# A transformer layer in split fp32: DMA queue in program order, stores on ScalarE's queue, weights loaded once with two products interleaved, the second norm begun early

## The chip, the cores and the metric

The kernel runs on one core of one Trainium2 chip. The metric is the device time in microseconds of one execution. Engines are named as in the profile: PE (TensorE, with PEld for its weight loads), DVE (VectorE), ACT (ScalarE), POOL (GpSimd), SP (SyncE, which only issues DMAs here).

## The reference

One layer over 512 latent tokens (width 2048) and 256 context tokens. A gated linear attention (4 heads, 128 wide keys, 256 wide values, scans in both directions from the context's final state) and a gated short convolution read the same normed, modulated input. One output projection, a second norm and a SwiGLU FFN with 5632 hidden columns follow, then a final norm. Cut to what matters:

```python
mx = silu(c) @ w_mod + b_mod                  # six rows: sh1, sc1, gt1, sh2, sc2, gt2
hx = rmsnorm(x, norm1_g) * (1 + sc1) + sh1    # the context likewise, from c_ctx
q, k, v, g, lf, lb, cb, cc, cx = split(hx @ w_in)
o = gla_forward(q, k, v, lf) + gla_backward(q, k, v, lb)
mix = concat([rmsnorm_per_head(o) * gla_g * silu(g), cb * conv3(cc * cx)]) @ w_out
x = x + gt1 * mix
h2 = rmsnorm(x, norm2_g) * (1 + sc2) + sh2
x = x + gt2 * ((silu(h2 @ w_ffn_gate) * (h2 @ w_ffn_up)) @ w_ffn_down)
out = rmsnorm(x, final_g)
```

Everything is fp32.

## The kernel before, in words

**Split products.** A product of fp32 matrices is three matmuls of halves (`mm3`, L79 to L84): each operand is split into a rounded half `hi`, made by an ACT copy (L96), and a rest `lo`, made by a DVE subtraction (L97) with both inputs in SBUF. Weights come from HBM as 512 KB tiles `raw` (128 x 1024, four buffers), and are split into `whi` and `wlo` (three buffers each); DVE and ACT do this once for every 12 matmuls of 512 columns.

**Stages**, in the profiled execution. 0 to 150 us: key projection; beside it each chunk of the input is scaled (`scaled_chunk`), whose factors come from small products with the modulation weights (`mod_cols`, tiles `pm`, `tm`, `pc`). 150 to 342: two value passes; the second also makes the shift's share (`shares`). 342 to 425: context states, q, gates. 425 to 875: the four heads, their chunked scan woven with the projections for gate, q and convolution; at each weave step `mod_some(MOD_STEP)` adds rows of the remaining modulation. A row is two 512 KB loads (`raw<-wm`) and two DVE reductions (L363); there are 64 rows. A head ends with a norm whose factors DVE makes in a chain of tiny operations (`rs_m`, `rs_t`, `rs_r`, L136 to L142), then ACT scales (`on`, L623) and PE transposes (`pt`, L629). 875 to 1050: output projection in two blocks of 1024 columns. 1050 to 1150: second norm and the first up block. To 1950: the FFN's 11 gate and up blocks (`wu`). To 2475: the down projection in GROUPS of 6, 6, 6 and 4 pairs of hidden tiles (`wd`), each twice, for the two halves of the columns; the results are added into 16 tiles `y`. Then the final norm and stores.

**Seven products.** From the output projection on, a product of 2 x 2 blocks is made by `seven` (L725 on): seven block products instead of eight, in the order u1 (A11), v (S1), u2 (S2), c12 (S4), u3 (S3), c11 (A12), c21 (A22). `prep_a` makes the left operands: sums and differences of blocks on DVE (tile `s`, L707 to L722) and their splits, named `a0` to `a6`, with `h` and `l`. The right ones are differences made on DVE in the tile `ch` (four buffers, L749 to L762) from weights loaded again for each product: of the eight loads for a unit, block 0 comes once, block 1 twice, block 2 twice, block 3 three times. Between the products, callbacks take the sums from PSUM; in the down stage they are additions `y += acc` on DVE (L974, one input in PSUM), and copies on ACT for the first group (L972). `norm2` runs after the output projection for tokens 0 to 255 and, for the rest, behind the first product of the first up block (`between`).

**Order.** The scheduler that builds the program orders each engine's instructions by their data, their buffers and its own estimates, DMA issues on SP among them; the order in the code is only a starting point. All DMAs, stores too, are issued by SP, which blocks while a target buffer isn't free. SBUF tiles of 2 KB per partition come from `xpool` (72), others from `fpool`; PSUM is three banks for accumulators and five for the rest.

Of the kernel before, what the change touches and what calls it, by code (L numbers as in the profile page):

```python
# [33 lines left out]
GROUPS = (6, 6, 6, 4)  # L34
EPS = 1e-6
# [16 lines left out]
def tile_hybrid_block(  # L52
# [11 lines left out]
    xpool = ctx.enter_context(tc.tile_pool(name="xpool", bufs=72))  # L64
    pspool = ctx.enter_context(tc.tile_pool(name="pspool", bufs=1, space=bass.MemoryType.PSUM))
# [148 lines left out]
    def scaled_chunk(i):  # L214
# [12 lines left out]
        for n, src, acc, dst, q in ((SEQ, xt, saccx, hx, 0), (CTX, ct, saccc, hc, 1)):  # L227
            if q == 0:
                hi, lo = (xpool.tile([P, n], F32R, tag="t", name=name) for name in ("hhi", "hlo"))
# [139 lines left out]
    MOD_STEP = 0.95  # L369
# [49 lines left out]
    for i in range(KD):  # L419
# [256 lines left out]
    fpool = ctx.enter_context(tc.tile_pool(name="fpool", bufs=1, side="right"))  # L676
    A11, S1, S2, S4, S3, A12, A22 = range(7)

    def f2k(name):
        return fpool.tile([P, NB], F32, tag="e", name=name, bufs=8)  # L680
# [4 lines left out]

    def a_unit(A, i, u):
        if A[i][u] is None:
            A[i][u] = tuple(xpool.tile([P, 2, HALF], F32R, tag="t", name=f"a{i}{p}") for p in "hl")
        return A[i][u]

    def prep_a(A, pieces):


        tmp = {}

        def put(n, i, src):
            hi, lo = a_unit(A, i, pieces[n][0])
            split(hi[:, pieces[n][1], :], lo[:, pieces[n][1], :], src)

        tt = nc.vector.tensor_tensor  # L700
        for n, (u, sel, a11, a12, a21, a22) in enumerate(pieces):
            put(n, A11, a11())
        yield
        for n, (u, sel, a11, a12, a21, a22) in enumerate(pieces):
            if u not in tmp:
                tmp[u] = xpool.tile([P, 2, HALF], F32, tag="t", name="s")
            tt(tmp[u][:, sel, :], a21(), a22(), op=ALU.add)  # L707
            put(n, S1, tmp[u][:, sel, :])
        yield
        for n, (u, sel, a11, a12, a21, a22) in enumerate(pieces):  # L710
            t = tmp[u][:, sel, :]
            tt(t, t, a11(), op=ALU.subtract)
            put(n, S2, t)
        yield
        for n, (u, sel, a11, a12, a21, a22) in enumerate(pieces):
            t = tmp[u][:, sel, :]
            tt(t, a12(), t, op=ALU.subtract)  # L717
            put(n, S4, t)
        yield
        for n, (u, sel, a11, a12, a21, a22) in enumerate(pieces):  # L720
            t = xpool.tile([P, 2, HALF], F32, tag="t", name="s3")[:, sel, :]
            tt(t, a11(), a21(), op=ALU.subtract)  # L722
            put(n, S3, t)
        yield
        for n, (u, sel, a11, a12, a21, a22) in enumerate(pieces):  # L725
            put(n, A12, a12())
        yield
        for n, (u, sel, a11, a12, a21, a22) in enumerate(pieces):
            put(n, A22, a22())
        yield  # L730

    def seven(A, wsrc, nk, after, between=lambda n: None):


        nu = nk // 2
        chain = [None] * nu
        tt = nc.vector.tensor_tensor

        def raw(b, u):
            return load_raw(wsrc(b, u))  # L740

        def b11(u):
            r = fpool.tile([P, 2 * NB], F32, tag="ch", name="ch", bufs=4)
            nc.sync.dma_start(r, wsrc(0, u))
            chain[u] = r
            return r

        def t1(u):
            tt(chain[u], raw(1, u), chain[u], op=ALU.subtract)  # L749
            return chain[u]  # L750

        def t2(u):
            tt(chain[u], raw(3, u), chain[u], op=ALU.subtract)  # L753
            return chain[u]

        def t3(u):
            r, r2 = raw(3, u), raw(1, u)
            tt(r, r, r2, op=ALU.subtract)  # L758
            return r

        def t4(u):
            tt(chain[u], raw(2, u), chain[u], op=ALU.subtract)  # L762
            return chain[u]

        X, Y, Z = [], [], []
        plan = (
            ("u1", A11, b11, X, abank, True), ("v", S1, t1, Y, bank, True), ("u2", S2, t2, X, None, False),
            ("c12", S4, lambda u: raw(3, u), Y, None, False), ("u3", S3, t3, X, None, False),
            ("c11", A12, lambda u: raw(2, u), Z, bank, True), ("c21", A22, t4, X, None, False),
        )  # L770
        for n, (name, i, src, acc, alloc, first) in enumerate(plan):
            if first:
                acc += [alloc("acc"), alloc("acc")]
            for u in range(nu):
                r = src(u)
                hi = wpool.tile([P, 1024], F32R, tag="whi", name="whi", bufs=3)
                lo = wpool.tile([P, 1024], F32R, tag="wlo", name="wlo", bufs=3)
                split(hi, lo, r)
                for t in range(2):
                    for k in range(2):  # L780
                        mm3(acc[t], sl(A[i][u], ALL, k, slice(t * P, t * P + P)),
                            (hi[:, k * NB : k * NB + NB], lo[:, k * NB : k * NB + NB]),
                            first and u == 0 and k == 0, u == nu - 1 and k == 1)
            after[name](acc)
            between(n)

    def sums(take):
# [4 lines left out]
        def copied(name):  # L792
            def f(acc):
                s[name] = [f2k(name) for _ in range(2)]
                for t in range(2):
                    nc.scalar.copy(s[name][t], acc[t])
# [16 lines left out]
    def cols_to_row(a, name):  # L813

        pt = bank("ptr")
        nc.tensor.transpose(pt[:KD, :P], modv[:, a : a + KD], ident)
        t = fpool.tile([KD, P], F32, name=name)
        nc.scalar.copy(t, pt[:KD, :P])
        row = tc.dram_tile([1, D], F32, name=name + "d")
        nc.sync.dma_start(row.rearrange("a (k p) -> (a k) p", p=P), t)  # L820
        return row

    def bcast(row, d):
        t = big()
        nc.sync.dma_start(t, row[0, d * NB : d * NB + NB].partition_broadcast(P))
        return t
# [6 lines left out]
    for _ in prep_a(A, [(k // 2, k % 2, mx(8 + k, 0), mx(k, 0), mx(8 + k, 1), mx(k, 1)) for k in range(8)]):  # L833
# [4 lines left out]
    for p in range(NBD // 2):  # L838
        gb = [bcast(gt1d, 2 * p + c) for c in range(2)]
        for tt in range(NX):  # L840
            for c in range(2):
                xn[tt][2 * p + c] = big()
                nc.sync.dma_start(xn[tt][2 * p + c], xr[tt, :, (2 * p + c) * NB : (2 * p + c) * NB + NB])

        def take(tt, c, t, acc):
            d = 2 * p + c
            if t is None:
                t = f2k("g21")
# [272 lines left out]
```

## Time and profile before

| what | value |
|---|---|
| median of the 3 runs shown | 2504.96 us (2496.47 to 2507.55) |
| profiled execution, its own time | 2495.26 us |
| its span | 2492.5 us |
| granted TensorE clock, mean | 0.967 |
| PE busy | 2299.3 us (92%), 10184 matmuls |
| DVE, ACT, POOL busy | 1737.6 (70%), 1029.4 (41%), 72.8 us (3%) |
| moved by DMA | 523.16 MB, 210 GB/s over the span |
| weight loads of 512 KB for output, up and down | 64, 352, 176 |

A row of the timeline gives start, duration, engine, line, operation, out<-in, shape and count; in brackets the idle time just before it and what ended it. A row of the waits gives engine and line, what it waited for, the total, how often, and the longest. A row of a group gives the busy time, the mean in ns, then idle time before. Sums over PE's rows include time at half clock, so a busy PE is not one at full speed; the granted clock tells that apart.

### The profile page before, as it was taken

How to read it: one execution, taken by the hardware profiler on the slowest of the kernel's cores; microseconds unless marked ns; L12 is line 12 of the kernel's file. 1: busy time of each engine (PE TensorE's matmuls, PEld its weight loads, DVE VectorE, ACT ScalarE, POOL GpSimd, SP SyncE). 2: the span in 40 equal slices, each digit the busy share in tenths (PEclk: the TensorE clock that was granted, in tenths of full speed). 3: DMA queues.
4: the chain of work that ended last, by engine and by line, in shares of the span. 5: the costliest groups of instructions: out<-in, count | busy, mean ns of one | idle time of the engine just before them, and what ended most of it. 6: DMA issues, size and time to landing. Idle time of an engine off the chain costs nothing. (4 is left out here: it accounts for less than half of the span.)

```text
span 2492.5 us, 27479 instructions
## 1 busy us (share of the span) xinstructions
PE 2299.3 (92%) x10184; PEld 1806.4 (72%) x10184; DVE 1737.6 (70%) x2140; ACT 1029.4 (41%) x1388; POOL 72.8 (3%) x77
## 2 busy tenths in 40 slices
PE   7899999898989978979999999999999889799996
PEld 4565666777867867767788887887788667687874
DVE  3356255665656488698677876777667677799998
ACT  3333146233222354465444444444444444444443
POOL 2223000000000000000000000000000000000000
PEclk9999999999989999989999999999999989899998
DMA  8655366566756448637666776667666856576684
GB/s 287 220 191 175 110 216 205 195 212 195 234 186 214 132 160 281 217 102 245 215 212 211 253 239 204 215 214 254 225 203 213 262 168 221 186 252 218 223 285 143
DMA packets 183586, 523.16 MB, mean 210 GB/s; under 512 B 18907, under 2 KB 50939, under 8 KB 183324
## 3 DMA queue, kind: packets, MB, share of 16 engines
q1 hardware_dynamic: 183452, 521.42, 64.4%
q8 instruction: 79, 1.29, 0.2%
q14 instruction: 55, 0.45, 0.1%
HBM read 501.40 MB, written 19.94 MB: 209 GB/s over the span
## 5 line engine op out<-in xcount | busy, mean ns | idle before, releaser
L96 ACT CAST whi<-raw 128x1024 fp32r<-128x1024 f32 x318 | 332.2, 1050 | 624.6 <-PE acc L84 327.3
L97 DVE TENSOR_TENSOR wlo<-raw,whi 128x1024 fp32r<-128x1024 f32 x318 | 391.0, 1235 | 255.8 <-ACT whi L96 254.7
L96 ACT CAST whi<-ch 128x1024 fp32r<-128x1024 f32 x296 | 310.5, 1050 | 349.7 <-PE acc L84 251.1
L97 DVE TENSOR_TENSOR wlo<-ch,whi 128x1024 fp32r<-128x1024 f32 x296 | 360.3, 1220 | 90.9 <-ACT whi L96 88.5
L84 PE MATMUL acc<-hhi,wlo 128*128 128x512 f32 x640 | 257.7, 410 | 17.6 <-DVE wlo L97 9.5
L363 DVE CUSTOM_DVE_ANT_0 raw<-raw,cbc 128x1024 f32<-128x1024 f32 x128 | 156.2, 1224 | 166.7 <-DMA raw<-wm 165.1
L84 PE MATMUL acc<-hlo,whi 128*128 128x512 f32 x640 | 256.3, 401 | 0.3 <-DVE hlo L102 0.3
L84 PE MATMUL acc<-hhi,whi 128*128 128x512 f32 x640 | 254.9, 398 | 0.0
L84 PEld LDWEIGHTS acc<-hhi,wlo 128*128 128x128 f32 x640 | 122.3, 192 | 49.9 <-ACT hhi L101 9.0
L84 PEld LDWEIGHTS acc<-hlo,whi 128*128 128x128 f32 x640 | 123.6, 193 | 28.3 <-issue 1.9
L84 PEld LDWEIGHTS acc<-hhi,whi 128*128 128x128 f32 x640 | 123.6, 193 | 27.9 <-issue 1.9
L84 PE MATMUL acc<-whi,a2l 128*128 128x512 f32 x296 | 117.4, 400 | 17.5 <-ACT big L972 10.0
L84 PE MATMUL acc<-whi,a0l 128*128 128x512 f32 x296 | 117.5, 398 | 16.2 <-DVE a0l L97 16.2
L84 PE MATMUL acc<-wlo,a1h 128*128 128x512 f32 x296 | 120.6, 407 | 12.4 <-DVE wlo L97 12.4
L84 PE MATMUL acc<-wlo,a6h 128*128 128x512 f32 x296 | 118.7, 401 | 13.3 <-DVE wlo L97 13.3
L84 PE MATMUL acc<-wlo,a4h 128*128 128x512 f32 x296 | 119.1, 402 | 12.7 <-DVE wlo L97 12.5
L84 PE MATMUL acc<-whi,a4l 128*128 128x512 f32 x296 | 117.0, 399 | 9.5 <-ACT whi L96 6.1
L84 PE MATMUL acc<-wlo,a0h 128*128 128x512 f32 x296 | 118.0, 399 | 8.1 <-DVE wlo L97 8.1
L758 DVE TENSOR_TENSOR raw<-raw 128x1024 f32<-128x1024 f32 x74 | 90.5, 1223 | 47.7 <-DMA raw<-wu 32.3
L84 PE MATMUL acc<-whi,a1l 128*128 128x512 f32 x296 | 118.0, 404 | 5.8 <-DVE a1l L97 3.9
L84 PE MATMUL acc<-wlo,a2h 128*128 128x512 f32 x296 | 117.0, 395 | 2.7 <-DVE wlo L97 2.6
L84 PE MATMUL acc<-whi,a1h 128*128 128x512 f32 x296 | 118.9, 402 | 0.0
(277 smaller groups left out, 4590.7 us busy)
## 6 DMA issues: line engine op xcount, KB each, us to landing
raw<-wu SPq DMA_DIRECT2D x308, 512.0 KB, 4.4
raw<-wd SPq DMA_DIRECT2D x154, 512.0 KB, 4.5
raw<-wm SPq DMA_DIRECT2D x128, 512.0 KB, 4.8
raw<-wo SPq DMA_DIRECT2D x56, 512.0 KB, 4.7
raw<-wc SPq DMA_DIRECT2D x48, 512.0 KB, 4.0
ch<-wu SPq DMA_DIRECT2D x44, 512.0 KB, 5.6
big<-wsc SPq DMA_DIRECT2D x64, 256.0 KB, 6.0
big<-wsh SPq DMA_DIRECT2D x64, 256.0 KB, 5.5
```

Of the source, the lines that this page charges most:

```text
L84: nc.tensor.matmul(o, l, r, start=start, stop=stop, skip_group_check=True)
L96: nc.scalar.copy(hi, src)
L97: (eng or nc.vector).tensor_tensor(lo, src, hi, op=ALU.subtract)
L363: nc.vector.tensor_tensor_reduce(out=w, in0=w, in1=cbc[:, hf * 1024 : hf * 1024 + 1024], scale=1.0, scalar=0.0, op0=ALU.mult, op1=ALU.add, ...
L758: tt(r, r, r2, op=ALU.subtract)
```

## The change

- **Weights once.** `seven` now loads each weight block once per unit, holds the blocks it needs again (`held`, eight buffers), and runs in five steps: "1" is u1, "5" is v, "63" is u2 and c12 interleaved by unit from the same loaded block, "7" is u3, "24" is c11 and c21 interleaved. Loads per unit go from eight to four: 36, 180 and 90 for output, up and down (some blocks run the last step as "2" and "4" apart, which loads block 2 twice). The number of matmuls stays.
- **SP in program order.** The scheduler no longer moves SP's instructions. Stores of the FFN's activations, of the residual (`xnd`) and of two rows go to ACT's queue (62 in all); the output's stay on SP.
- **Modulation rows.** `mod_some(1, 16)` in the second value pass moves 16 of the 64 rows there; `MOD_STEP` goes from 0.95 to 0.7.
- **Output projection.** Its contraction is paired anew (`MIX1`, `MIX2`), so that the first product needs neither the last heads nor the last convolution tiles.
- **Second norm.** Tokens 0 to 255 go through it before step "7" of the second output block, the rest are scaled behind that block and transposed before step "5" of the first up block.
- **Down stage.** The 44 operand sums of its groups are made on POOL, and 82 of the additions into `y` are an ACT copy from PSUM and a POOL addition of two SBUF tiles.
- **Buffers.** PSUM is one pool of eight banks from the output projection on; `xpool` has 56 tiles, `fpool` 17 of its kind; right halves of odd chunks in the first projection use the buffers that later hold `ch`.

```diff
+MIX1, MIX2 = (8, 9, 10, 11, 0, 1, 2, 3), (12, 13, 4, 5, 14, 15, 6, 7)
-    xpool = ctx.enter_context(tc.tile_pool(name="xpool", bufs=72))
+    xpool = ctx.enter_context(tc.tile_pool(name="xpool", bufs=56))
...
-    MOD_STEP = 0.95
+    MOD_STEP = 0.7
...
             for k in ((2 * i - 12, 2 * i - 11) if i < 12 else (i,)):
                 shares(k)
+        mod_some(1, 16)
...
+    ps2 = ctx.enter_context(tc.tile_pool(name="ps2", bufs=8, space=bass.MemoryType.PSUM, reuse_waits="tile"))
...
+        def held(bl, u):
+            r = wpool.tile([P, 2 * NB], F32, tag="ch", name="ch", bufs=8)
+            nc.sync.dma_start(r, wsrc(bl, u))
             return r
...
+        for step in steps:
+            if step in before:
+                before[step]()
             for u in range(nu):
+                end = u == nu - 1
+                if step == "1":
+                    a[u] = held(0, u)
+                    product(A11, u, a[u], X, True)
...
+                elif step == "5":
+                    b[u] = held(1, u)
+                    tt(a[u], b[u], a[u], op=ALU.subtract)
+                    product(S1, u, a[u], Y, True)
...
+                elif step == "63":
+                    d = load_raw(wsrc(3, u))
+                    tt(a[u], d, a[u], op=ALU.subtract)
+                    product(S2, u, a[u], X, False)
...
+                    product(S4, u, d, Y, False)
+                    tt(b[u], d, b[u], op=ALU.subtract)
...
+                elif step == "7":
+                    product(S3, u, b[u], X, False)
...
+                    c = load_raw(wsrc(2, u))
+                    if "2" in step:
+                        product(A12, u, c, Z, True)
...
+                    if "4" in step:
+                        tt(a[u], c, a[u], op=ALU.subtract)
+                        product(A22, u, a[u], X, False)
...
+        before = {"63": load_x}
+        if p:
+            before["7"] = half_a
+        seven(A, lambda b, u: wo[p, b, u], 8, sums(take, True), ("1", "5", "63", "2", "7", "4") if p else ALL_STEPS, before)
...
+        if j == 0:
+            steps, before = ("1", "2", "5", "63", "7", "4"), {"5": half_b}
...
-        nc.sync.dma_start(actd[4 * j + q], t)
+        nc.scalar.dma_start(actd[4 * j + q], t)
...
-        for _ in prep_a(A, pieces):
+        for _ in prep_a(A, pieces, eng=nc.gpsimd):
...
+                        elif fast:
+                            nc.vector.tensor_tensor(o, o, acc[t], op=ALU.add)
                         else:
-                            nc.vector.tensor_tensor(o, o, acc[t], op=ALU.add)
+                            s = big()
+                            nc.scalar.copy(s, acc[t])
+                            nc.gpsimd.tensor_tensor(o, o, s, op=ALU.add)
...
-    with tile.TileContext(nc) as tc:
+    with tile.TileContext(nc) as tc, tc.manual_schedule(engines={mybir.EngineType.SP}):
```

`fast` is the second block of the last group; it keeps its additions on DVE.

**What moves on the engines.** First PE in the key projection, at one of its pairs of chunks: `pm` are the modulation products, `pc` the small one behind the copy `tm`, `acc` with `chl` the context's products, `acc` with `hhi` those of the next scaled chunk. Before:

```order
L84 MATMUL pm<-big,silsh 32x256 x2
L84 MATMUL acc_99<-whi,chl 128x512
L84 MATMUL pm<-big,silsh 32x256 x8
L84 MATMUL pc<-smt,tm 128x2 x2
L84 MATMUL acc_94<-hhi,wlo 128x512
```

and now:

```order
L87 MATMUL pm<-big,silsh 32x256 x2
L87 MATMUL acc_101<-whi,chl 128x512
L87 MATMUL acc_101<-wlo,chl 128x512
L87 MATMUL acc_101<-whi,chl 128x512
L87 MATMUL pc<-smt,tm 128x2 x2
L87 MATMUL acc_100<-whi,chl 128x512
L87 MATMUL acc_101<-whi,chl 128x512
L87 MATMUL acc_96<-hhi,wlo 128x512
```

Three context products have come between the last `pm` and `pc`, and two between `pc` and the next chunk.

Second, DVE at the end of head 0, in the chain that makes the norm's factors; the ISA rows are the reductions of a modulation row. Before:

```order
L136 TENSOR_SCALAR rs_m<-ss 128x4
L138 RECIPROCAL rs_r<-rs_t 128x4
L139 TENSOR_TENSOR rs_t<-rs_r 128x4
L140 TENSOR_TENSOR rs_t<-rs_t,rs_m 128x4
L141 TENSOR_SCALAR rs_t<-rs_t 128x4
L363 ISA raw,modacc<-raw,cbc 128x1024
L363 ISA modacc 128x1
L142 TENSOR_TENSOR rs_r<-rs_r,rs_t 128x4
```

and now:

```order
L139 TENSOR_SCALAR rs_m<-ss 128x4
L141 RECIPROCAL rs_r<-rs_t 128x4
L142 TENSOR_TENSOR rs_t<-rs_r 128x4
L143 TENSOR_TENSOR rs_t<-rs_t,rs_m 128x4
L144 TENSOR_SCALAR rs_t<-rs_t 128x4
L145 TENSOR_TENSOR rs_r<-rs_r,rs_t 128x4
L370 ISA raw,modacc<-raw,cbc 128x1024
L370 ISA modacc 128x1
```

The reduction has gone behind the chain's last step. In head 2 it is the same; in head 1 a reduction stands inside the chain before and now.

Third, ACT at the start of the down stage's third group: `big<-acc` are the copies for the additions into `y`, `a0h` and `a1h` the new group's operands, `whi` its weights:

```order
L1015 COPY big<-acc 128x512 x4
L99 CAST a0h<-ar 128x512 x3
L99 CAST a1h<-s 128x512 x2
L99 CAST whi<-ch 128x1024
L99 CAST a1h<-s 128x512
```

and POOL at the same place:

```order
L1016 TENSOR_TENSOR y<-y,big 128x512 x28
L719 TENSOR_TENSOR s<-ar 128x512 x2
L721 TENSOR_TENSOR s<-s,ar 128x512
L719 TENSOR_TENSOR s<-ar 128x512
```

Before, ACT made no such copies there and POOL had no instruction in this stage: the additions into `y` (L974) and the sums `s` (L707 on) stood on DVE, spread among the weight splits. Now the sums `s` wait on POOL behind all additions of the group before.

More of the change, by code (lines that the diff above doesn't have):

```diff
@@ L790, in sums @@
+    def sums(take, roomy=False):
         s = {}
@@ L793, in f @@
             def f(acc):
-                s[name] = [f2k(name) for _ in range(2)]
+                s[name] = [big() if roomy and name == "v" else row2k(name) for _ in range(2)]
                 for t in range(2):
```

305 lines of the change are left out of this document (150 added, 155 removed).

## The prediction

> **What bounds the kernel now.** I read the page's head first, then the table of stretches that cut the span at the stages' borders, then the list of waits, and last the single rows around the longest waits. The head says that TensorE is the bound, and how nearly:
>
> ```profile
> span 2492.5 us, 27479 instructions
> PE 2299.3 (92%) x10184; PEld 1806.4 (72%) x10184; DVE 1737.6 (70%) x2140; ACT 1029.4 (41%) x1388; POOL 72.8 (3%) x77
> ```
>
> The table of stretches gives, for each, its length, the busy time of PE, PEld, DVE, ACT and POOL with their records, the granted clock, the share of the DMA engines and GB/s:
>
> ```profile
> 16.00:150.00 134.00, 120.05 (x632) 78.17 (x632) 49.58 (x77) 46.49 (x84) 39.16 (x42) 0.95 0.69 223
> 255.00:342.00 87.00, 87.00 (x406) 55.81 (x405) 20.36 (x32) 14.25 (x23) 2.34 (x3) 1.00 0.45 148
> 425.00:875.00 450.00, 408.20 (x1847) 339.31 (x1848) 266.56 (x449) 130.38 (x210) 0.00 (x0) 0.95 0.60 194
> 875.00:975.00 100.00, 79.74 (x322) 62.06 (x321) 83.16 (x133) 49.88 (x92) 0.00 (x0) 0.93 0.65 212
> 1050.00:1150.00 100.00, 80.31 (x359) 64.33 (x358) 92.78 (x136) 59.60 (x93) 0.00 (x0) 0.93 0.50 156
> 1150.00:1950.00 800.00, 790.99 (x3529) 646.73 (x3528) 585.33 (x540) 368.41 (x422) 0.00 (x0) 1.00 0.70 224
> 1950.00:2025.00 75.00, 52.22 (x208) 40.52 (x207) 55.22 (x66) 35.30 (x50) 0.00 (x0) 0.84 0.54 179
> 2025.00:2475.00 450.00, 417.65 (x1743) 334.39 (x1741) 394.14 (x448) 196.70 (x240) 0.00 (x0) 0.96 0.68 222
> ```
>
> Two stages leave nothing to win: the second value pass (255 to 342) and the gate and up blocks (1150 to 1950) have PE busy for 87.0 of 87 and 791.0 of 800 us at full clock. The latter gives the price of a product: 800 us / 3529 records = 0.227 us. What can be won lies where PE idles, and there the clock column falls too: 425 to 875 has 41.8 us of idle and, at 0.95, 450 x 0.05 = 22.5 us more, so an idle microsecond costs 1.54 there. In the down stage (2025 to 2475) it is 32.4 of idle and 18 of clock, 1.56. No stretch fills the DMA engines. So I price the change by idle taken from PE, times some 1.5, and ask of every saved load whether PE or DVE was waiting for it.
>
> **The change part by part.**
>
> *Key projection.* For every pair of chunks PE now waits twice, at the small product behind the modulation and at the next scaled chunk. The list of waits within 16 to 150 sums these:
>
> ```profile
> 94.33 0.61 PE L84 MATMUL pc<-smt,tm 128*128 128x2 f32 x4 [0.55 <-ACT tm L203]
> 96.12 1.36 PE L84 MATMUL acc<-hhi,wlo 128*128 128x512 f32 x4 [1.19 <-ACT hhi L101]
> PE acc L84 <- ACT hhi L101: 8.1, 7, 1.2
> PE pc L84 <- ACT tm L203: 4.3, 8, 0.6
> ```
>
> In the new PE order three context products stand between the last modulation product and the small one (3 x 0.227 = 0.68, more than 0.55), and two behind it (0.45 of 1.19). What remains is 8 x 0.74 = 5.9 of 12.4: 6.5 saved. The clock's loss there is 134 x 0.05 = 6.7; I count 5.5 of it. **+12**, between 6.5 (idle alone) and 19 (both gone).
>
> *Sixteen modulation rows moved into the second value pass.* They are 32 loads of 512 KB in a stretch that moved 148 GB/s x 87 = 12.9 MB, 24 loads. 56 loads are 29.4 MB. The fastest stretch of the trace is
>
> ```profile
> 0.00:50.00 50.00, 35.32 (x214) 20.60 (x215) 16.05 (x23) 17.68 (x32) 10.99 (x21) 0.99 0.94 302
> ```
>
> At 302 GB/s that is 97 us, at the 223 of 16 to 150 it is 132. With only four raw buffers I take 102, i.e. **-15**; -45 at the slow end, 0 if the scheduler's loads spread into the neighbours. DVE's 32 x 1.22 = 39 us of row reductions fit beside its 20.4 busy.
>
> *Attention heads.* All of PE's idle there is in three waits; the first two are
>
> ```profile
> PE pt L629 <- ACT on L623: 20.3, 3, 8.1
> PE psc L84 <- DVE qe L568: 16.4, 6, 4.8
> 513.38 1.22 DVE L363 CUSTOM_DVE_ANT_0 raw<-raw,cbc 128x1024 f32<-128x1024 f32 x1 [2.63 <-DMA raw<-wm]
> 514.53 0.16 DVE L142 TENSOR_TENSOR rs_r<-rs_r,rs_t 128x4 f32<-128x4 f32 x1
> 515.31 0.69 PE L629 MATMUL pt<-cidt,on 128*128 128x128 f32 x2 [5.76 <-ACT on L623]
> 736.30 2.42 PE L629 MATMUL pt<-cidt,on 128*128 128x128 f32 x8 [8.08 <-ACT on L623]
> 847.21 1.03 PE L629 MATMUL pt<-cidt,on 128*128 128x128 f32 x8
> ```
>
> In head 0 a modulation row, itself late by DMA, stands inside the norm's short chain on DVE, just ahead of its last step (L142), and PE waits 5.76 for it. In head 3, where no row is left to load, PE doesn't wait (847.21). The three waits are those of heads 0, 1 and 2. The new DVE order has the chain unbroken in heads 0 and 2 and still broken in head 1, so 5.76 + 8.08 = 13.8 go. Times 1.54 that is 21. DVE loses 39 of its 267 us there, 15%; I let the score waits shrink by as much, 2.4 x 1.54 = 4. **+25**, from 8 (one head, and nothing else) to 50.
>
> *Products of w_out.* Each weight block is loaded once, so the stage needs 36 loads for 64, and the inputs' halves are paired so that the first product needs no late head. But PE's long wait at its start is for DVE, which prepares the operands:
>
> ```profile
> 889.34 0.79 PE L84 MATMUL acc<-wlo,a0h 128*128 128x512 f32 x1 [7.72 <-DVE wlo L97]
> 902.87 0.80 PE L84 MATMUL acc<-wlo,a1h 128*128 128x512 f32 x1 [2.42 <-DVE wlo L97]
> ```
>
> The same operand splits still stand ahead of the third weight split in the new DVE order, so I leave these 10.1 us. The other 10.2 of the 20.3 idle in 875 to 975 I let go, with their share of the clock (7 x 10.2/20.3 = 3.5), less some 2 since all four units' operands of one kind now come in a row: **+12**, 0 to 20.
>
> *Norm begun early.* Its two waits are
>
> ```profile
> 1069.43 5.56 PE L885 MATMUL pt<-cidt,big 128*128 128x128 f32 x32 [5.30 <-ACT big L878]
> 1096.95 0.80 PE L84 MATMUL acc<-whi,a1l 128*128 128x512 f32 x1 [3.94 <-DVE a1l L97]
> ```
>
> Half a's transposes now have 48 products behind them before their result is read, and half b's 96 (A11 and A12). Both waits, 9.2, go; their clock share I set against what moves into the stage ahead: **+9**, -5 to 20.
>
> *Gate and up blocks.* Loads go from 352 to 180, but PE idles 9 of 800 us: **0**, at best +9, at worst -20 if buffers held longer stop something. The 62 stores on ACT's queue I count at nothing, since ACT is busy for 41% of the span; where they stand ahead of a cast that PE waits for, they are part of the -20.
>
> *Down stage.* Here DVE is busy 394 of 450 and PE waits for it. What goes:
>
> ```profile
> 1980.65 0.80 PE L84 MATMUL acc<-whi,a0l 128*128 128x512 f32 x1 [8.39 <-DVE a0l L97]
> 2015.55 0.79 PE L84 MATMUL acc<-whi,a2l 128*128 128x512 f32 x1 [9.97 <-ACT big L972]
> 2122.25 0.80 PE L84 MATMUL acc<-whi,a0l 128*128 128x512 f32 x1 [5.90 <-DVE a0l L97]
> 2140.79 0.47 PE L84 MATMUL acc<-whi,a2l 128*128 128x512 f32 x1 [2.79 <-DVE big L974]
> 2268.65 0.80 PE L84 MATMUL acc<-wlo,a1h 128*128 128x512 f32 x1 [2.25 <-DVE wlo L97]
> 2419.01 0.80 PE L84 MATMUL acc<-wlo,a6h 128*128 128x512 f32 x1 [3.45 <-DVE wlo L97]
> ```
>
> The first group's operands are now split among the last up block's weights; eight shared banks end the waits for a copied bank; the rest belong to group starts, priced anew below. Together 32.7 x 1.56 = 51. DVE is rid of 82 additions into y and 44 operand sums, 126 x 0.68 = 86 us. But POOL takes them, and the two engines block each other:
>
> ```profile
> L974 DVE TENSOR_TENSOR big<-big,acc 128x512 f32<-128x512 f32 x96 | 63.4, 680 | 1.8 <-PE acc L84 1.6
> L97 DVE TENSOR_TENSOR wlo<-ch,whi 128x1024 fp32r<-128x1024 f32 x296 | 360.3, 1220 | 90.9 <-ACT whi L96 88.5
> 199.81 1.29 POOL L294 TENSOR_TENSOR ht<-hhi,hlo 128x512 f32<-128x512 f32 x1 [1.23 <-PE pl L84]
> 199.87 2.32 DVE L97 TENSOR_TENSOR wlo<-raw,whi 128x1024 fp32r<-128x1024 f32 x1
> ```
>
> The split at 199.87, which begins just behind a POOL addition, takes 2.32 instead of its usual 1.22: 1.10 lost. All 126 would cost DVE 139 us. DVE without its additions is busy (394 - 86)/450 = 68%, nearly all of it with two operands in SBUF; I charge 0.68 x 139 = 95, net 9 us more on DVE, x 1.56 = -14. The Trainium skill's page "SBUF — State Buffer", section "Who interferes with whom", states that a VectorE instruction with two SBUF inputs and a GpSimd one that reads SBUF exclude each other for the whole instruction, while one with at most one SBUF input is free. By that rule the additions removed (one input in PSUM) never blocked and those added do; the rows at 199.8 agree.
>
> At the start of groups 2 to 4 the new ACT order has four copies, five operand casts (two of sums that POOL makes behind four y additions) and only then the first weight cast. From the last product: copies 2 x 0.63, one addition and two sums on POOL 3 x 1.29, two casts 1.2, the weight cast 1.05: some 8 us, and 3 x 8 x 1.56 = -37. Stage: 51 - 14 - 37 = **0**. If POOL blocked nothing, the 14 comes back, and with it the 15 us of other waits for weight splits (x 1.56 = 23): +37. If each addition blocks in full, (53 - 9) x 1.56 = -69.
>
> *End.* Row scaling of finished rows stood ahead of the last additions on DVE:
>
> ```profile
> 2474.54 0.39 PE L84 MATMUL acc<-whi,a6h 128*128 128x512 f32 x1
> 2471.81 5.39 DVE L996 SCALAR_TENSOR_TENSOR big<-big,rs_r 128x512 f32<-128x512 f32 x8
> 2477.11 1.28 DVE L974 TENSOR_TENSOR big<-big,acc 128x512 f32<-128x512 f32 x2
> ```
>
> The last product ends at 2474.9, its addition starts at 2477.1; in the new order the finished rows come earlier, and 2.2 us go: **+2**.
>
> Sum: 12 - 15 + 25 + 12 + 9 + 0 + 0 + 2 = 45. The profiled execution took 2495.3 us around its span of 2492.5, 9.7 below the median of the runs shown, 2504.96. So 2450 for it, and **2460** for the median.
>
> **The rivals.**
>
> *POOL's additions block DVE in full.* For it: the pair at 199.8, DVE's 88% in the down stage, and that both engines' operands lie in SBUF. Against: POOL's additions come in groups behind ACT's copies, and some must fall into DVE's waits for casts (88.5 us over all splits of held blocks). The stage loses 69 more: 2529, slower. It decides from 29 us of extra blocking, since 45 / 1.56 = 29, that is when the additions cost 95 + 29 = 124 of 139. The Trainium skill's page "SBUF — State Buffer", in the section named above, has whichever engine starts first hold the other off in full; the trace has four splits beside POOL and no whole stage, so it can't say how often they meet.
>
> *The order of SP takes it back.* Where SP goes in program order and waits for one of four raw buffers, all behind it wait. The second value pass then runs at 223 GB/s (-45 instead of -15), and a head's chain stays as late as its loads (0 instead of 25): 2460 + 30 + 25 = 2515, no change. For it: DVE waits for modulation rows over most of the heads:
>
> ```profile
> DVE raw L363 <- DMA raw<-wm: 165.1, 85, 4.9
> ```
>
> Against: the order on DVE in two heads has no row inside the chain.
>
> *POOL runs beside DVE for nothing.* Then DVE falls to two thirds of the down stage: 2460 - 37 = 2423.
>
> **How the numbers follow.** A measurement of this kernel tells about 0.5%, 12.5 us, from no change. Forecast 0.48 (its own range 2440 to 2488, all faster), full blocking 0.17, SP's order 0.15, free additions 0.20. So faster 0.68, same 0.15, slower 0.17. The range reaches into both sides' cases: 2412 to 2522.
>
> **What would show it.** Right: no wait of several us at the transposes of heads 0 and 2; the second value pass near 100 us with over 280 GB/s; the waits at 1069, 1980, 2015 and 2122 gone; weight splits in the down stage with a mean between 1.4 and 1.8 us instead of 1.22, and some 8 us of idle at the starts of groups 2 to 4. Wrong: a mean above 2 us there (full blocking), a value pass above 120 us, or idle in the blocks of 1150 to 1950, where I expect none.

## The result and the profile after

The changed kernel takes 2571.6 us (2568.3 to 2574.5), the kernel before 2500.7 in the same rounds: a ratio of 1.028, 95% interval 1.025 to 1.031. It is slower; the forecast was 2460, the range 2412 to 2522.

The table of stretches of the changed kernel shows where. Its borders are put where PE has done as much work (each matmul counted with its duration at full clock) as at the borders used before. The columns are those of the prediction's table.

```profile
0.00:191.00 191.00, 152.51 (x671) 90.61 (x672) 57.98 (x84) 49.01 (x93) 42.27 (x47) 0.84 0.55 176
191.00:314.00 123.00, 109.15 (x486) 66.72 (x485) 68.85 (x112) 32.20 (x53) 35.23 (x28) 0.93 0.52 181
314.00:421.00 107.00, 91.66 (x398) 58.45 (x397) 50.42 (x82) 15.28 (x25) 1.05 (x2) 0.89 0.73 247
506.00:920.00 414.00, 398.96 (x1852) 331.91 (x1852) 235.87 (x398) 131.38 (x212) 0.00 (x0) 0.99 0.54 174
2026.00:2573.00 547.00, 428.11 (x1744) 341.01 (x1742) 415.08 (x355) 242.54 (x328) 213.61 (x114) 0.89 0.32 110
```

(Some of these borders lie 1 us beside those of the next table, and the last row leaves out the down stage's first 54 us.)

The lengths of all stages of the two kernels, in us, each from its own profiled execution with borders set in that way, and each rounded by itself:

| stage | before | changed | forecast's gain | measured gain |
|---|---|---|---|---|
| key projection | 150 | 191 | +12 | -41 |
| first value pass | 105 | 122 | none named | -17 |
| second value pass | 87 | 108 | -15 | -21 |
| heads | 450 | 413 | +25 | +37 |
| output projection | 175 | 176 | +12 | -1 |
| second norm, first up block | 100 | 88 | +9 | +12 |
| gate and up blocks | 800 | 789 | 0 | +11 |
| down stage and end | 543 | 600 | +2 | -58 |

The remaining stretch (context states, 83) became 85. Two stretches carry the loss: everything up to the end of the second value pass, 79 us, and the down stage with its end, 58. The gains in between are 59. The two profiled executions lie 79 us apart, the medians 71, so some us of the table are differences between executions of one kernel.

In the heads the three waits at the transposes, 20.3 us in the kernel before, are nearly gone:

```profile
PE pt L637 <- ACT on L631: 3.4, 3, 1.5
```

**The key projection.** PE's timeline of the changed kernel has the same wait once in each pair of chunks, of which three are shown, with the stretches just behind the middle one:

```profile
53.64 1.19 PE L87 MATMUL acc<-whi,chl 128*128 128x512 f32 x2 [2.96 <-DVE chl L105]
74.15 1.19 PE L87 MATMUL acc<-whi,chl 128*128 128x512 f32 x2 [2.88 <-DVE chl L105]
94.06 1.19 PE L87 MATMUL acc<-whi,chl 128*128 128x512 f32 x2 [2.96 <-DVE chl L105]
76.00:78.00 2.00, 2.00 (x6) 1.55 (x5) 1.32 (x1) 0.00 (x0) 1.91 (x2) 0.50 0.53 174
80.00:82.00 2.00, 2.00 (x15) 1.10 (x14) 0.00 (x0) 0.00 (x0) 0.00 (x0) 1.00 0.00 0
```

The period is 19.9 to 20.5 us; before it was about 16.4 (79.68 to 96.12). The wait is 2.9 us where the two waits before made 1.7, and five microseconds at half clock follow it. What PE waits for is `chl`, the scaled context chunk of the *next* pair.

From the first of these waits to the last it is 121.5 us for six periods, where the kernel before took 96.5: 25 of the 41 us. Most of the rest, 14, is lost behind the last wait (35.3 us to the stage's border, 20.9 before). There PE waits for the norm's factors and for the first weights of the next stage:

```profile
171.16 0.71 PE L87 MATMUL pr<-rb_d,cidt 128*128 128x128 f32 x4 [2.32 <-DVE rb_d L152]
175.91 1.22 PE L87 MATMUL acc<-whi,hlo 128*128 128x512 f32 x2 [1.41 <-ACT whi L99]
179.97 0.79 PE L87 MATMUL acc<-wlo,hhi 128*128 128x512 f32 x1 [2.85 <-DVE wlo L100]
```

The loads of these weights were issued at 138 us; their cast stands on ACT behind the copies of the factors (L288), at 174.8. Before, products of the value pass stood between these factors' products, and PE didn't wait.

**The down stage.** PE's waits from the second group on:

```profile
2121.39 1.22 PE L87 MATMUL acc<-whi,a0l 128*128 128x512 f32 x2 [4.21 <-ACT whi L99]
2140.57 0.80 PE L87 MATMUL acc<-wlo,a1h 128*128 128x512 f32 x1 [5.04 <-DVE wlo L100]
2158.85 0.79 PE L87 MATMUL acc<-whi,a2l 128*128 128x512 f32 x1 [6.55 <-ACT big L1015]
2271.82 1.22 PE L87 MATMUL acc<-whi,a0l 128*128 128x512 f32 x2 [7.01 <-ACT whi L99]
2434.57 1.22 PE L87 MATMUL acc<-whi,a0l 128*128 128x512 f32 x2 [19.98 <-ACT whi L99]
2476.03 1.22 PE L87 MATMUL acc<-whi,a5l 128*128 128x512 f32 x2 [7.63 <-ACT whi L99]
2497.11 1.22 PE L87 MATMUL acc<-whi,a0l 128*128 128x512 f32 x2 [8.30 <-ACT whi L99]
2551.06 1.22 PE L87 MATMUL acc<-whi,a6l 128*128 128x512 f32 x2 [17.48 <-ACT whi L99]
```

The first four belong to the starts of groups 2 and 3, which the forecast had priced at 8 us each; they have three waits each (15.8 us in the second group, 18.6 in the third, of which one is shown). The last four, 53 us, are in the last group: its start, priced at 8 as well, and three waits that the forecast had not named. Three lists tell what stands behind the first and the last of them. First ACT at 2414, the start of the last group:

```profile
2414.68 0.58 ACT L1015 COPY big<-acc 128x512 f32<-128x512 f32 x1 [0.77 <-PE acc L87]
2415.16 1.14 ACT L99 CAST a0h<-ar 128x512 fp32r<-128x512 f32 x2
2418.31 0.62 ACT L99 CAST a1h<-s 128x512 fp32r<-128x512 f32 x1 [2.00 <-POOL s L719]
...
2432.43 1.13 ACT L99 CAST a6h<-ar 128x512 fp32r<-128x512 f32 x2
2433.47 1.99 ACT L99 CAST whi<-ch 128x1024 fp32r<-128x1024 f32 x2
```

All 14 operand casts stand ahead of the group's first weight cast, with a wait for a POOL sum before most of them. The waits at 2476 and 2497 end in the same manner: ACT's weight cast stands behind Squares of finished blocks (L1029), which wait for DVE and, through it, for POOL's additions:

```profile
2473.71 0.63 ACT L1029 ACTIVATE big<-y 128x512 f32<-128x512 f32 x1 [3.86 <-DVE y L1028]
2474.95 1.03 ACT L99 CAST whi<-raw 128x1024 fp32r<-128x1024 f32 x1
```

Second SP at the end, and third the groups of POOL's additions and of DVE's weight splits:

```profile
2481.11 0.85 SPq L1026 DMA_DIRECT2D big<-xnd  x2
2536.77 4.97 SPq L1037 DMA_DIRECT2D out<-y  x8
2542.83 0.88 SPq L115 DMA_DIRECT2D raw<-wd  x2
```

```profile
L1016 POOL TENSOR_TENSOR y<-y,big 128x512 f32<-128x512 f32 x82 | 157.2, 1936 | 277.0 <-ACT big L1015 276.5
L100 DVE TENSOR_TENSOR wlo<-ch,whi 128x1024 fp32r<-128x1024 f32 x370 | 478.2, 1300 | 148.5 <-ACT whi L99 147.0
L100 DVE TENSOR_TENSOR wlo<-raw,whi 128x1024 fp32r<-128x1024 f32 x244 | 312.9, 1283 | 108.9 <-ACT whi L99 108.6
```

SP issues nothing between 2482 and 2536.8: it stands at the stores of the first finished rows, whose values are not there yet, and the last two weight loads come behind them. POOL's addition takes 1.94 us in the mean, where the kernel before had 1.29; the splits are 0.06 to 0.08 longer, which is (1.300 - 1.222) x 370 + (1.283 - 1.227) x 244 = 43 us against the kernel with the additions on DVE (below). In the window from 2026 us on alone, the splits take 1.48 us in the mean, within the 1.4 to 1.8 that the prediction had named:

```profile
L100 DVE TENSOR_TENSOR wlo<-ch,whi 128x1024 fp32r<-128x1024 f32 x102 | 151.1, 1486 | 40.5 <-ACT whi L99 40.2
L100 DVE TENSOR_TENSOR wlo<-raw,whi 128x1024 fp32r<-128x1024 f32 x42 | 61.9, 1475 | 25.6 <-ACT whi L99 25.6
```

### The profile page after: what moved, and what is told of

Its sections match the earlier page's. It is cut to its first block, busy times and chain, and to the rows that moved or that the text cites. A ratio compares the mean times of both kernels' runs of the same rounds, so it can differ in the third digit from the quotient of the medians.

```text
span 2572.6 us, 27050 instructions
## 1 busy us (share of the span) xinstructions
PE 2328.3 (91%) x10184; PEld 1820.3 (71%) x10184; DVE 1743.1 (68%) x2014; ACT 1070.9 (42%) x1471; POOL 313.9 (12%) x203
## 5 line engine op out<-in xcount | busy, mean ns | idle before, releaser
L100 DVE TENSOR_TENSOR wlo<-ch,whi 128x1024 fp32r<-128x1024 f32 x370 | 478.2, 1300 | 148.5 <-ACT whi L99 147.0
L719 POOL TENSOR_TENSOR s<-ar 128x512 f32<-128x512 f32 x11 | 18.8, 1715 | 1618.7 <-DMA ar<-actd 1618.7
L87 PE MATMUL acc<-hhl,whi 128*128 128x512 f32 x640 | 201.6, 395 | 0.0
L1016 POOL TENSOR_TENSOR y<-y,big 128x512 f32<-128x512 f32 x82 | 157.2, 1936 | 277.0 <-ACT big L1015 276.5
L87 PE MATMUL acc<-hhi,wlo 128*128 128x512 f32 x320 | 140.1, 438 | 5.5 <-DVE wlo L100 5.5
L87 PEld LDWEIGHTS acc<-hhl,whi 128*128 128x128 f32 x640 | 119.7, 189 | 33.5 <-issue 9.5
L87 PE MATMUL acc<-wlo,a0h 128*128 128x512 f32 x296 | 121.9, 412 | 20.0 <-DVE wlo L100 19.9
L87 PE MATMUL acc<-whi,a6l 128*128 128x512 f32 x296 | 117.1, 397 | 19.3 <-ACT whi L99 17.5
L87 PE MATMUL acc<-hlo,whi 128*128 128x512 f32 x320 | 132.2, 413 | 0.0
L87 PE MATMUL acc<-hhi,whi 128*128 128x512 f32 x320 | 131.2, 410 | 0.0
L87 PE MATMUL acc<-hhl,wlo 128*128 128x512 f32 x320 | 126.6, 395 | 0.0
L87 PE MATMUL acc<-whi,a5l 128*128 128x512 f32 x296 | 117.0, 396 | 7.6 <-ACT whi L99 7.6
```

What stands on the lines that cost most here:

```text
L87: nc.tensor.matmul(o, l, r, start=start, stop=stop, skip_group_check=True)
L100: (eng or nc.vector).tensor_tensor(lo, src, hi, op=ALU.subtract)
L1016: nc.gpsimd.tensor_tensor(o, o, s, op=ALU.add)
```

## The experiments

All edits are to the changed kernel, and all times are medians beside the kernel before (2497 to 2500 in these rounds).

**SP's issues placed by the scheduler.**

```diff
-    with tile.TileContext(nc) as tc, tc.manual_schedule(engines={mybir.EngineType.SP}):
+    with tile.TileContext(nc) as tc:
```

> The changed kernel with one part undone: the scheduler again places SP's DMA issues (no program order on SP). Theory: program order on SP makes the scheduler see the modulation weights of the key projection late, so that PE waits 2.9 us for the context's scaled chunk in every pair (19.9 us a pair) and runs at half clock behind it; and it puts the stores of the first finished rows ahead of the last weight loads, for which PE waits 17.5 us at 2551. Then the part up to the end of the second value pass (421 us in the changed kernel, 342 before) falls by 50 to 80 us, the 17.5 us wait goes, and the time is 2480 to 2510. Rival: the smaller tile pool and the odd chunks' halves in other buffers slow that part; then it stays at 400 us or more, and the time is 2545 to 2575.

Measured 2486.2, ratio 0.996 (0.994 to 0.997): 85 us less. The key projection is at 150 us again, the first value pass at 110; the second stays at 107. The end's wait of 17.5 us is down to 6.2. Its first 150 us read like those of the kernel before (228 GB/s there too, 672 products):

```profile
0.00:150.00 150.00, 127.14 (x672) 82.99 (x672) 55.35 (x85) 53.26 (x95) 39.48 (x47) 0.94 0.70 228
```

So the program order of one DMA queue, and not the tile pools, cost the projections 54 us (41 and 13). The down stage with its end takes 567 us instead of 600; PE's waits above 1.5 us in the last group fall from 56 us to 25, while those at the starts of groups 2 and 3 get no shorter.

**Additions and sums back on DVE.**

```diff
-        for _ in prep_a(A, pieces, eng=nc.gpsimd):
+        for _ in prep_a(A, pieces):
...
-                            s = big()
-                            nc.scalar.copy(s, acc[t])
-                            nc.gpsimd.tensor_tensor(o, o, s, op=ALU.add)
+                            nc.vector.tensor_tensor(o, o, acc[t], op=ALU.add)
```

> The changed kernel with one part undone: the additions into y and the operand sums of the down stage back on DVE, the additions reading PSUM, without ACT copies. Up to the down stage nothing changes. Theory A: what costs there is the serial chain at the starts of groups (copies on ACT, additions on POOL, sums on POOL, then the casts and only then the weight cast), with ACT in order behind it; then the waits at 2121, 2271, 2434, 2476 and 2497 (4.2, 7.0, 20.0, 7.6, 8.3 us) shrink and the time is 2500 to 2530. The 17.5 us wait for the last weights stays. Theory B: the lock between POOL and DVE costs more than the chain; then weight splits fall from 1.30 to 1.22 us, and the time falls by 60 us or more with PE's waits for DVE gone. Rival: the waits at group starts come from SP's program order (late loads); then they stay at 15 us or more in the last group and the time is 2555 to 2575.

Measured 2478.1, ratio 0.992 (0.990 to 0.994): 93 us less, more than theory A gave and within theory B's 60 or more. Down stage and end take 509 us instead of 600. No wait at a group start is above 2.2 us (the one at the start of the last group's second block is 4.3), and the splits are at 1.22. Both theories' signs came, so this run doesn't tell chain and lock apart; the experiments on the additions below do. The last group's wait for its last weights, SP's doing, stayed:

```profile
2116.16 0.50 PE L87 MATMUL acc<-wlo,a1h 128*128 128x512 f32 x1 [2.10 <-DVE wlo L100]
2230.58 0.79 PE L87 MATMUL acc<-wlo,a0h 128*128 128x512 f32 x1 [2.06 <-DVE wlo L100]
2355.09 0.50 PE L87 MATMUL acc<-wlo,a0h 128*128 128x512 f32 x1 [2.20 <-DVE wlo L100]
2453.94 1.22 PE L87 MATMUL acc<-whi,a6l 128*128 128x512 f32 x2 [18.49 <-ACT whi L99]
```

**The first stores behind the last product.** The eight stores of `out[0]` and `out[1]` are moved from `finish_rows` to behind the loop over the groups.

> The changed kernel with the eight stores of the first two finished token tiles issued behind the last product instead of ahead of it. Theory: SP, in program order, waits for these rows (54.7 us) and issues the last two weight loads and residual loads only then; with the stores behind, PE's 17.5 us wait at the end falls below 5 and the time is 2550 to 2560. Rival: the last product waits for DVE's final work anyway, time unchanged within 5 us of 2571.

Measured 2565.7, ratio 1.027 (1.025 to 1.029). The 17.5 us wait fell to 2.6 and a new one of 5.1 for the last split came behind it: ten microseconds off PE, but only 6 off the median, outside the expected 2550 to 2560, and the intervals of the two kernels overlap (1.025 to 1.031 for the changed one). Part of what the stores had held up was late for DVE's sake anyway. So the stores explain at most a part of the 33 us that SP's order costs in the down stage; its effect on the other waits of the last group was not taken apart.

**The modulation rows as before.** `MOD_STEP = 0.95`, and no `mod_some(1, 16)`.

> The changed kernel with the modulation rows as before (none in the second value pass, step 0.95 in the heads). Forecast's step: the moved rows cost the second value pass 15 us and win 25 in the heads. If so the time rises by 5 to 15, to 2580. Theory after the result: the second value pass lost 20.6 us and the heads won 37; undoing gives back 15 to 20 in the pass and takes 20 to 37 in the heads: 2570 to 2590. Rival: the heads won by other parts (SP's order, buffers) and the pass lost by the loads: the time falls by 10 to 20, to 2555.

Measured 2580.3, ratio 1.032 (1.030 to 1.034). The second value pass is back at 86 us, 22 less, and the heads at 447, 34 more. PE's waits at the transposes are back at 17.7 us. The moved rows thus win about 9 us, though the intervals of the two kernels still touch; and nearly all of the 37 us in the heads is theirs.

**Both parts undone.** The first two edits together.

> The changed kernel with both parts undone: SP's issues placed by the scheduler, and the down stage's additions and sums on DVE. Theory: the two costs lie in different stages (SP's order in the projections and at the end, POOL's chain in the down stage), so the gains add: 2571 - 85 - 93 = 2393, within 12. Rival: they share a cost (the last group, where both held weights back), then 2405 to 2440.

Measured 2400.7, ratio 0.961 (0.957 to 0.964): 171 us less where the two gave 85 and 93. The costs are nearly independent.

**The modulation weights one chunk earlier, SP still in program order.** `mod_cols` is cut in two, and its loads for the next pair are issued in the odd chunk ahead:

```diff
+        if i + 1 in sc_at and i > 1:
+            fetch_cols(wsc, i + 1, sc_at[i + 1])
         xt = big()
         nc.sync.dma_start(xt, xT[:, i, :])
```

In the order of PE the small product then has all of the odd chunk's products behind it:

```
MATMUL pm<-big,silsh 32x256 x14
MATMUL pc<-smt,tm 128x2 x2
MATMUL acc_96<-hhl,wlo 128x512
```

> The changed kernel, SP still in program order, but in the program each pair's modulation weights of the key projection are loaded one chunk earlier. Theory: not program order itself but the late place of these loads in it makes the scheduler spread the modulation products and put the small product just before its result is needed. In the order of this kernel the modulation products stand together and a whole odd chunk's products stand behind the small one, so PE's 2.9 us waits in each pair go, the key projection ends at 150 to 160 us instead of 191, and the time is 2530 to 2542. Rival: the 56 tiles limit how far loads run ahead; then the loads wait for tiles, and the key projection stays at 180 us or more.

Measured 2528.4, ratio 1.012 (1.010 to 1.015): 43 us less, and the key projection ends at 151. The waits for `chl` are 6.6 us in all, where the seven of the changed kernel (2.9 each) make 20.4:

```profile
PE acc L87 <- DVE chl L105: 6.6, 7, 2.9
PE pc L87 <- ACT tm L219: 4.2, 8, 0.6
```

So the waits in the pairs came not from program order itself but from the place that these loads had in it. A pair now takes 13.8 us from the second on, less than the 16.1 of the kernel before. Behind the last pair nothing changed: the waits of 2.3, 1.4 and 2.9 us are still there, and this part takes 32 us. With SP's issues scheduled they are absent (22 us for this part), so some 10 us remain a price of program order, by way of the order on ACT.

**The additions alone, the sums alone.** First only the additions into `y` back on DVE, then only the operand sums.

> The changed kernel with the additions into y back on DVE; the operand sums stay on POOL. Theory of the chain: without additions ahead of them, POOL's sums are ready early, ACT has no copies ahead of the casts, and the waits at group starts (15 to 20 us each) go: 2475 to 2500, nearly as with both undone (2478). Rival, lock by count of POOL instructions (82 of 126): two thirds of the 93 us, about 2510.

> The changed kernel with the operand sums back on DVE; the additions into y stay on POOL behind ACT copies. Theory of the chain: the sums no longer queue behind the additions, so the 20 us wait of the last group falls below 8, but copies still stand ahead of the casts and the Square of the last group still waits for POOL: 2520 to 2545. Rival, lock by count (44 of 126): a third of the 93 us, about 2540, with the waits for casts unchanged. If the chain through the sums were all of it, the time would be that with both undone, 2478.

Measured 2489.0 (0.996, 0.994 to 0.998) and 2545.5 (1.019, 1.017 to 1.021). Undone alone, the additions are worth 83 of the 93 us, the sums 26; 44 sums left on POOL cost 11 us (the two kernels' intervals just touch), 82 additions 67. The expectation that the 20 us wait would fall below 8 with the sums on DVE was wrong: it stayed at 18.8. The queue of sums behind additions on POOL was not what held the weight cast.

**POOL's traffic without its place.** Additions and sums on DVE, and behind each addition but the fast block's one on POOL that nobody reads: `nc.gpsimd.tensor_tensor(scratch, o, o, op=ALU.add)`.

> The kernel with both additions and sums on DVE (2478), and behind each of the 82 additions into y one more addition on POOL, of two SBUF operands, whose result nobody reads: POOL's traffic without its place in the chain. If what y's additions on POOL cost (2546 against 2478, 67 us) is the lock between the engines, the time is 2525 to 2550 with weight splits at 1.27 us. If it is the chain of copy, addition and what waits for them, the lock shows in the splits (1.25 to 1.27) and costs at most 20 us: 2478 to 2498.

Measured 2506.2, ratio 1.003 (1.002 to 1.005): 28 us more than without, between the two expectations. The lock in its groups:

```profile
L100 DVE TENSOR_TENSOR wlo<-ch,whi 128x1024 fp32r<-128x1024 f32 x370 | 460.1, 1250 | 121.4 <-ACT whi L99 119.6
L1015 POOL TENSOR_TENSOR scratch<-y 128x512 f32<-128x512 f32 x82 | 127.8, 1559 | 1952.6 <-DVE y L1013 1948.8
```

28 / 82 = 0.34 us of time for each addition, where the prediction's row at 199.87 has a split lose 1.10 beside one.

**The path by copies without POOL.** Sums on DVE, and `nc.vector` in place of `nc.gpsimd` in the addition; the ACT copy stays.

> The changed kernel with sums on DVE and the additions into y on DVE too, but still by way of an ACT copy, from two SBUF operands: the chain's copies without POOL. If the copies ahead of the casts on ACT are what the starts of groups wait for, some 5 us remain at each and the time is 2495 to 2515. If it is POOL's slow additions (1.9 us each) that hold back copies' tiles and the last group's Square, the time is 2470 to 2490.

Measured 2526.2, ratio 1.010 (1.008 to 1.013): 48 us more than with additions straight from PSUM, beyond both expectations. POOL is not needed for the long wait; ACT's order at the last group is the same as in the changed kernel:

```profile
2376.79 0.58 ACT L1015 COPY big<-acc 128x512 f32<-128x512 f32 x1 [0.77 <-PE acc L87]
2377.28 1.14 ACT L99 CAST a0h<-ar 128x512 fp32r<-128x512 f32 x2
2379.94 0.62 ACT L99 CAST a1h<-s 128x512 fp32r<-128x512 f32 x1 [1.53 <-DVE s L719]
...
2392.60 1.13 ACT L99 CAST a6h<-ar 128x512 fp32r<-128x512 f32 x2
2393.64 1.99 ACT L99 CAST whi<-ch 128x1024 fp32r<-128x1024 f32 x2
2394.73 1.22 PE L87 MATMUL acc<-whi,a0l 128*128 128x512 f32 x2 [17.97 <-ACT whi L99]
```

In the kernel whose additions read PSUM, ACT's casts are spread among the weight casts of the group before:

```profile
2326.22 0.61 ACT L99 CAST a0h<-ar 128x512 fp32r<-128x512 f32 x1
2327.98 1.06 ACT L99 CAST whi<-ch 128x1024 fp32r<-128x1024 f32 x1 [1.15 <-PE acc L87]
...
2331.66 0.61 ACT L99 CAST a1h<-s 128x512 fp32r<-128x512 f32 x1
```

With copies, the scheduler puts the next group's operands behind the last copies. Why it does was not tried; its view of ACT's load or of the copies' tiles may decide it.

The kernels so far make a chain in which each differs from the one before by one edit: additions by way of copies, on DVE (2478.1 to 2526.2, 48 us), the same additions on POOL (to 2545.5, 19 us), the sums on POOL as well (to 2571.6, 26 us). Together these are the 93. The parts are sure to some 3 us, since they come from different rounds.

**Program order kept, its costs out.** The edits on the loads, the stores, the additions and the sums together.

> SP still in program order, with the modulation weights of the key projection loaded one chunk earlier, the first finished rows stored behind the last product, and additions and sums on DVE. Gains measured one by one: 43, 6 to 14 and 93 us. If they add: 2571 - 142 to 150 = 2421 to 2429. What then stays above the kernel with SP's issues scheduled (2401) is the first value pass, 12 to 17 us.

Measured 2425.9, ratio 0.971 (0.968 to 0.974), as the single gains add. (Of its parts, the stores' 6 is not clear of noise.) The first value pass is at 121 us against 114 with SP's issues scheduled, and the down stage with its end takes 501 against 485.

**Scheduled, and the loads ahead.** Both parts undone, and the modulation weights one chunk earlier.

> SP's issues placed by the scheduler, additions and sums on DVE (2401), and the key projection's modulation weights one chunk earlier in the program. If their place in the program still decides, the 1.1 us waits of each pair and the half clock behind them go, and the time is 2375 to 2392; if the scheduler places them by itself, 2401 within 8.

Measured 2389.1, ratio 0.956 (0.954 to 0.958), the best version of the study. The key projection takes 137 us; of the 1.1 us waits per pair that were left only the first two remain (1.1 and 1.8). The 14 us to the kernel with these loads ahead and SP in program order (151) are mostly the part behind the last pair, where PE doesn't wait now. The place in the program decides even where the scheduler may move the loads.

## Why the prediction was wrong, by its own steps

**Key projection, +12: the sign was wrong.** The step read the two context products behind `pc` as work of the old chunk that would cover 0.45 us of the next chunk's wait. They belong to the next pair and need its `chl`, which is made behind `gx`, `hhi` and `hlo`; PE meets the chain earlier, not later. A wait of 2.9 us per pair instead of 1.7, followed by half clock, gave 25 of the 41: over the six periods PE idles 17.5 us instead of 11.3, and the granted clock is 0.84 instead of 0.93, some 13 us; what makes the remaining 6 was not measured. The other 14, behind the last pair, were no term of the sum. The names in the order alone did not tell to which pair of chunks a product belongs. Undoing the queue's order brings the stage back to 150 us, moving its loads by one chunk to 151.

**SP in program order.** It was priced only in a rival, and there for the second value pass and the heads. That rival's place was wrong and its mechanism half right: the second pass takes 107 us with and without program order, and the heads won all the same. Undoing it won 41 and 13 us in the projections and 33 in the down stage. For the pairs of the key projection the runs show why: the loads' place. In the last group SP stood for 54.7 us at stores of unfinished rows, but moving these won 6 us, not clear of noise; why the first value pass paid 13 was not tried. What is queued behind each waiting issue on SP should have been read; the forecast did that for ACT and POOL only.

**Second value pass, -15, and heads, +25: right in kind.** -21 and +37. The pass moved 247 GB/s, less than the 280 assumed. The heads' waits at the transposes fell by 16.9 us and not by 13.8: head 1's, which the forecast had left, went as well. The granted clock is 0.99 instead of 0.95. The rows taken out give 34 of the 37, as the run with them put back shows.

**Output projection, +12: -1.** The loads saved were not what PE waited for: its wait for the operands' splits at the start, which the forecast left at 7.7, grew to 12.2 (at 940 us), and its waits in the stage are 24 us in all, as before.

**Norm, +9: +12; gate and up, 0: +11.** The first number is near by luck: of the two waits that were to go, the one for the transposes (5.30) went, but the one for `a1l` (3.94) is still there, 4.39 at 1145.6; shorter waits for splits, which the forecast had not counted, made up for it. In gate and up PE's idle time fell from 9.0 to 3.6 us, and its busy time, which the forecast took as fixed, from 791.0 to 785.4, so the gain is above the 9 that it called the best. No run has the weights loaded again or the norm late with all else kept, so these gains are read off the profiles.

**Down stage, 0: about -58 with the end.** The gains at the first group came (21 us). The step that failed is the group starts at 37 us: it took one order (four copies, five casts, the weight cast) for three groups, 8 us each. For the second and third the first wait was below that price (4.2 and 7.0), but two more of 5 and 6.5 us followed in each; for the fourth the order has 14 casts ahead of the weight cast, which the forecast did not look at, and the wait was 20. The end's +2 was wrong in the same manner: in the last group Squares on ACT and stores on SP stand ahead of weights, 33 us in three waits.

**The lock, -14: right in kind, too small.** The splits' mean in the stage, 1.48 us, is as forecast, and below the 2 us that would have been the sign of full blocking. In time the lock cost more than 14: 28 us for 82 additions (the unread ones), 11 for the 44 sums alone on POOL, 39 together, though the second figure has the sums' own lateness in it. The charge on DVE, 95 us, was not too small (the splits, the largest part, lost 43); what failed is that 86 us taken off DVE would pay for it. With the additions straight from PSUM on DVE the waits at the group starts are short, so DVE's total was not what PE waited for. The Trainium skill's page "SBUF — State Buffer", section "Who interferes with whom", says who blocks whom; the splits beside POOL agree (1.48 us, 1.22 without). But the lock is under half of the 93 us. The rival that had the loss on this side, full blocking at 2529, had the right sign and stage and the wrong mechanism: the path by copies alone costs 48 us without any POOL instruction.

## What to carry to other kernels

A DMA queue in program order makes the program's text the schedule: each issue that must wait (for a free tile, for a row to be stored) holds every load behind it, so loads that feed a chain belong earlier in the text (one chunk earlier was worth 43 us here). Stores of unfinished results belong behind the last load, though here that won at most a few us. Work moved from a busy engine to an idle one is paid in the queues that it passes: follow, on each in-order engine, what the new copies stand ahead of, at every border of groups or stages (the last group alone had 53 us of such waits). An order of one border is no evidence for the next.

## What was not expected of the hardware

A wait of 2.9 us on PE is followed by about 5 us at half clock (granted clock 0.50, 0.50 and 0.56 in the three stretches from 74 to 80 us), so that it costs nearly twice its length. In the kernel before, the two waits of a pair (0.55 and 1.18 us) were followed by it in some pairs (from 79.7 us on) and not in others (at 64.6). The Trainium skill's page "TensorE: Matmul & The Clock Gate", section "What's actually happening", gives an idle window of about 3.4 us for the clock to fall, and here shorter waits did it. POOL suffers from the lock as well: its addition of 128 x 512 takes 1.29 us in the mean in the kernel before, 1.56 with nobody waiting for it and 1.94 in the changed kernel, 8.7 at most. And in the up blocks, where the loads fell from 352 to 180 and the DMA engines' share from 0.70 to 0.38, the time went from 800 to 789 us only.
